# Dealing the context's attention units among the latent ones, and taking two norms as columns

## The chip, the cores and the metric

One core of one Trainium2 chip runs the whole kernel. The metric is device time in microseconds (us) from the start to the end of one execution; lower is better. A profiled execution also gives a span, from the core's first instruction to its last, and a trace of every instruction on TensorE (PE, with its weight loads as PEld), VectorE (DVE), ScalarE (ACT), GpSimd (POOL) and the DMA queues, of which SP's is one.

## The reference

The network has two layers, over a prefix of 256 context tokens and 1024 latent tokens, 1024 features wide. Layer 0 is windowed attention, layer 1 a Mamba-2 mixer. The part that matters here is layer 0 and the norm in front of layer 1:

```python
u = rms_normalize(h) * (1.0 + scale[:, None]) + shift[:, None]      # before each layer, h latent or context
# layer 0, a block of 128 latent queries: keys of up to 3 neighbouring blocks and all 256 context keys
s = jnp.einsum('bqkgd,bskd->bkgqs', qb, kb).astype(jnp.float32) * scale
p = sink_softmax(s, sink_kg, mask).astype(vb.dtype)
o = jnp.einsum('bkgqs,bskd->bqkgd', p, vb)
# the context's queries: the 256 context keys alone
s = jnp.einsum('bqkgd,bskd->bkgqs', q_c, k_c).astype(jnp.float32) * scale
p = sink_softmax(s, sink_kg, None).astype(v_c.dtype)
# both: gate, output projection, gated residual
y = (o * jax.nn.silu(g)) @ w_out
h = h + gate[:, None] * y
```

`rms_normalize` multiplies each token by one over the square root of the mean of its squares plus 1e-6. There are 16 query heads in 4 groups; each group shares one key/value head.

## The kernel before

Features lie on the partitions, tokens on the free axis. The tokens are three tiles: tile 0 and tile 1 are latent tokens 0 to 511 and 512 to 1023, tile 2 is the context (256). Every fp32 product is made of three fp32r matmuls, from a high part and a low part of each operand (`mm3`, lines 220 to 226: a high weight by high data, a low weight by high data and a high weight by low data). The low parts are made by subtraction: for weights on GpSimd (`split_w`, line 212), after a cast on ScalarE (line 210).

**Units.** Attention runs over 40 units, one for each of 10 blocks of 128 queries (blocks 0 to 3 are tile 0, 4 to 7 tile 1, 8 and 9 the context) and each of 4 key/value heads `j`. A unit has a front (`att_front`): the scores `S` of 4 query heads on TensorE (lines 670 for latent keys, 671 for context keys), mask and row minimum on VectorE (674), the exponential on ScalarE (676). It has a back (`att_back`): for each block of keys, 4 transposes into `pt` (695), a copy to `ph` on ScalarE (699), the low part `pl` on VectorE (700), and two matmuls into `pv` (701, 702). Then come two transposes of the reciprocal sums (708), the gate (709), the copy `co` (711), the sum `ot` (714), the product with the gate on GpSimd (715), and high and low part of the result (717, 718). A latent unit has 4 or 5 blocks of keys, a context unit has 2. The front of the next unit is traced ahead of the back of this one (`AHEAD = 1`).

**Fillers.** Between the key blocks of the units stand parts of projections that don't depend on them. `tick`, called once per key block, hands out `total * seen / count` parts. Each part is 3 matmuls with a moving operand of 512 columns (256 for tile 2's output), 8 parts (24 matmuls) make one projection into the single PSUM bank `pj`. Each projection loads two half weights on SP's queue and splits them. The list is in three stages: beside the 8 context units 5 projections (`QC`) of tile 1's queries; beside the 16 units of tile 0 the other 3 queries and 8 gates of tile 1; beside the 16 units of tile 1 the output projections of tile 2 and then of tile 0 (`out_steps`). Query projections end in the rotary rotation (lines 532 to 553), gate projections in a tanh and one VectorE instruction (571, 572).

**Norms.** After its 8 output projections a tile has the residual stream in DRAM (`h_d`) and the sum of squares in `acc`. `fin` makes the norm: `rstd` multiplies `acc` by a matrix of ones on TensorE (256), so that all 128 partitions hold the sum, then takes a square root on ScalarE (258) and a reciprocal on VectorE (259) of the whole tile. `modulate` then reads `h_d` back in 8 pieces, through two buffers `h1`, and makes high and low part of the normed input of layer 1 (291 to 293). Both are done for tile 2 and for tile 0 during or at the end of the units of tile 1.

**After the units** come the output projections of tile 1 (8, on alternating banks), a small projection for the time steps of the context (`dt_context`), the norm of tile 1 (`rstd_last`, which takes sums of squares as columns, line 796, and the power -1/2 on GpSimd, line 800) and layer 1.

**What sets the order.** The code is traced once; a scheduler then orders each engine's instructions by its own estimate of their times, by priority (fillers have a lower one) and by a few forced orders (`issue_after`). The result is a fixed sequence per engine; each engine takes its instructions in that order and waits at one whose inputs are not there.

## Time and profile before

| | us |
|---|---|
| runs of the kernel before: median (lowest to highest, 3 runs) | 1783.06 (1781.8 to 1784.47) |
| the profiled execution's own time | 1781.34 |
| its span | 1779.6 |
| TensorE busy in the span | 1727.1 (97%) |
| VectorE, ScalarE, GpSimd busy | 1172.5, 840.8, 808.4 |
| units of the context, from the first score matmul to the last units' end | about 260 to 336 |
| units of tile 0 | to about 508 |
| units of tile 1 | to about 701 |

The stage times are read off the trace where the gate's product (line 709) of the last unit of each stage runs. Busy TensorE is not TensorE at its peak: a matmul's record includes the time it takes to pass through the array, so one that stands alone shows 0.39 us where a stream of the same ones takes one every 0.23 us. The busy time of the weight loads (PEld), one for each matmul and of 0.19 us for most, tells more about how dense the stream is.

### The profile page before, as it was taken

The numbers are of one execution on the slowest core, as the hardware profiler recorded it, in microseconds if no ns is written. First come the engines' busy times: TensorE is split into PE (matmuls) and PEld (weight loads), VectorE is DVE, ScalarE is ACT, GpSimd is POOL, SyncE is SP. The second block draws the span as 40 slices with busy tenths as digits, with TensorE's granted clock in tenths as the row PEclk, the third lists the DMA queues.
The fourth block names the chain that finished last, engine by engine and source line by source line (L and its number), as shares of the span: only waits on it lengthen the run. The fifth ranks groups of instructions, "written<-read, shape, count | busy, mean of one in ns | idle before, by whom it ended". The sixth has DMA issues, their size and how long they took to land.

```text
span 1779.6 us, 28767 instructions
## 1 busy us (share of the span) xinstructions
PE 1727.1 (97%) x10115; PEld 1479.3 (83%) x10115; DVE 1172.5 (66%) x2174; ACT 840.8 (47%) x1769; POOL 808.4 (45%) x1070
## 2 busy tenths in 40 slices
PE   6999998999999899999999999999999999999997
PEld 3797767788889787789898898989889898987886
DVE  3563436787777766585776758677675866876643
ACT  3532226677778766453443434344343443443533
POOL 2441117654456465403455463635545464554222
PEclk9999999999999999999999999999999999999999
DMA  8758866553445444412333333233333333565533
GB/s 302 284 148 258 265 190 148 124 130 85 101 119 130 119 143 151 164 47 64 86 78 90 80 79 83 78 92 72 95 81 80 83 77 88 167 174 161 179 106 119
DMA packets 261617, 227.89 MB, mean 128 GB/s; under 512 B 84704, under 2 KB 201312, under 8 KB 260448
## 3 DMA queue, kind: packets, MB, share of 16 engines
q1 hardware_dynamic: 227408, 207.40, 39.8%
q0 software_dynamic: 34064, 18.65, 5.8%
q8 instruction: 80, 1.31, 0.3%
q14 instruction: 65, 0.53, 0.1%
HBM read 191.14 MB, written 35.13 MB: 127 GB/s over the span
## 4 chain that ended last, share of the span: by engine, by line
PE 85%; DVE 5%; issue 3%; DMA 3%; ACT 2%; POOL 1%; SPq 0%; DVEq 0%; POOLq 0%; ACTq 0%
PE pj L1182 19%; PE pj L1218 10%; PE pj L224 6%; PE pj L226 6%; PE pj L225 6%; PE pj L1664 4%; PE psD L1199 4%; PE pt L695 3%; PE psX L1365 3%; PE psD L1278 2%; PE pv L702 2%; PE pv L701 2%; PE S L670 2%; PE psX L1338 1%; PE psX L1337 1%
## 5 line engine op out<-in xcount | busy, mean ns | idle before, releaser
L224 PE MATMUL pj<-uH,wh 128*128 128x512 f32 (+1 forms) x572 | 212.6, 372 | 5.5 <-DVE rope_b L533 2.3
L226 PE MATMUL pj<-uH,wl 128*128 128x512 f32 (+1 forms) x572 | 200.2, 350 | 0.1
L225 PE MATMUL pj<-uL,wh 128*128 128x512 f32 (+1 forms) x572 | 199.7, 349 | 0.0
L212 POOL TENSOR_TENSOR wl<-wr,wh 128x512 fp32r<-128x512 f32 x92 | 121.3, 1321 | 98.5 <-ACT wh L210 97.0
L1182 PE MATMUL pj<-uH,wl 128*128 128x512 f32 x480 | 163.3, 407 | 0.0
L1182 PE MATMUL pj<-uH,wh 128*128 128x512 f32 x480 | 163.1, 411 | 0.0
L1182 PE MATMUL pj<-uL,wh 128*128 128x512 f32 x480 | 162.3, 408 | 0.0
L700 DVE TENSOR_TENSOR pl<-pt,ph 128x512 fp32r<-128x512 f32 x168 | 114.2, 687 | 60.6 <-ACT ph L699 59.8
L1218 PE MATMUL pj<-wh,uL 128*128 128x256 f32 x512 | 152.3, 297 | 0.0
L1218 PE MATMUL pj<-wh,uH 128*128 128x256 f32 x512 | 152.0, 297 | 0.0
L1218 PE MATMUL pj<-wl,uH 128*128 128x256 f32 x512 | 151.8, 296 | 0.0
L224 PEld LDWEIGHTS pj<-uH,wh 128*128 128x128 f32 x572 | 108.2, 189 | 32.9 <-issue 8.4
L674 DVE CUSTOM_DVE_ANT_0 sm<-S,mask,nsink 128x640 f32<-128x640 f32 (+2 forms) x160 | 118.8, 772 | 25.4 <-PE S L671 13.6
L210 ACT CAST wh<-wr 128x512 fp32r<-128x512 f32 (+1 forms) x132 | 84.8, 645 | 94.9 <-PE pj L225 68.0
L699 ACT CAST ph<-pt 128x512 fp32r<-128x512 f32 x168 | 97.4, 585 | 63.7 <-PE pt L695 58.1
L676 ACT ACTIVATE sm<-sm,nm 128x640 f32<-128x640 f32 (+2 forms) x160 | 118.6, 742 | 11.7 <-DVE nm L674 11.4
L226 PEld LDWEIGHTS pj<-uH,wl 128*128 128x128 f32 x572 | 108.0, 189 | 16.5 <-issue 1.7
L225 PEld LDWEIGHTS pj<-uL,wh 128*128 128x128 f32 x572 | 108.5, 190 | 12.4 <-issue 2.5
L1255 POOL TENSOR_TENSOR xw<-xn,dtdec 128x256 f32<-128x256 f32 x144 | 91.7, 641 | 55.3 <-PE psD L1278 31.4
L1373 POOL TENSOR_TENSOR ss<-ss,half 128x1 f32<-128x1 f32 x64 | 43.0, 672 | 160.3 <-ACT y L1372 160.2
L1331 POOL TENSOR_TENSOR xs<-xn,sk 128x256 f32<-128x256 f32 x64 | 46.2, 722 | 134.7 <-DVE sk L1329 134.6
L1182 PEld LDWEIGHTS pj<-uL,wh 128*128 128x128 f32 x480 | 90.4, 188 | 18.3
(415 smaller groups left out, 4994.0 us busy)
## 6 DMA issues: line engine op xcount, KB each, us to landing
fd<-acs SPq DMA_DIRECT2D x64, 256.0 KB, 4.9
bd<-acs SPq DMA_DIRECT2D x64, 256.0 KB, 4.9
wr<-w_x SPq DMA_DIRECT2D x31, 512.0 KB, 3.7
wr<-w_sk SPq DMA_DIRECT2D x24, 512.0 KB, 4.1
wr<-wg SPq DMA_DIRECT2D x44, 256.0 KB, 4.4
qs<-q POOLq DMA_DIRECT2D x40, 256.0 KB, 3.9
wr<-wo SPq DMA_DIRECT2D x40, 256.0 KB, 2.7
wada<-w_ad SPq DMA_DIRECT2D x8, 1024.0 KB, 6.4
```

Of the source, the lines that this page charges most:

```text
L210: nc.scalar.copy(h, raw)
L212: (eng or nc.vector).tensor_tensor(l, raw, h, op=ALU.subtract)
L224: self.nc.tensor.matmul(ps, lh, rh, start=first and i == 0, stop=False)
L225: self.nc.tensor.matmul(ps, lh, rl, start=False, stop=False)
L226: self.nc.tensor.matmul(ps, ll, rh, start=False, stop=last and i == n - 1)
L674: nc.vector.tensor_tensor_reduce(out=sm[:, :W], in0=Sv, in1=self.mask[:, m0 : m0 + W], scale=-SCALE, scalar=self.nsink[:, 4 * j + r : 4 * ...
L676: nc.scalar.activation(sm[:, :W], sm[:, :W], AF.Exp, bias=nm[:, r : r + 1], scale=-1.0, accum_out=sums[:, r : r + 1])
L699: nc.scalar.copy(ph, ptf)
L700: nc.vector.tensor_sub(pl, ptf, ph)
L1182: nc.tensor.matmul(raw[:, 512 * i : 512 * i + 512], l[:, k, :], r[i][:, k, :], start=k + y == 0, stop=k == KT - 1 and y == 2)
L1218: nc.tensor.matmul(pj[:, c], l, r[:, k, :], start=c % 2 + q + k + y == 0, stop=c % 2 == 1 and q == 1 and k == 3 and y == 2)
L1255: nc.gpsimd.tensor_tensor(xw, X(st, c).rearrange("p (r h) -> p r h", r=R), self.dtdec[:, c, hd(d, g)].unsqueeze(2).broadcast_to([P, R, HP] ...
```

## The change

Three things are changed, and two constants with them.

1. The list of units. The 8 context units no longer come first: each is followed by two units of tile 0. The fillers beside these 24 units are one list (8 queries, then 8 gates), handed out by weight: a key block of a context unit counts twice (`load`). `QC` is no longer used, and the second list's `count` is 2 larger, so that a few of its steps are left for the flush after the last unit.
2. The norms of tiles 2 and 0. The sums of squares are taken as columns (one matmul with one column per 128 tokens), scaled on VectorE, raised to -1/2 by GpSimd; in a second step, matmuls with the columns broadcast as weights and the identity as moving operand spread them over the partitions, and ScalarE copies the result. The square root, the reciprocal and the matmul by ones are gone there. The modulation (`rescale`) becomes a generator of 8 steps, and `aside` takes one of them after each filler part; what is left after the last unit is done at once.
3. `dt_context` is put behind the matmuls of the fourth output projection of tile 1, as these were traced last.

```diff
-SLACK = (0, 0, 0)
+SLACK = (0, 2)
...
+            def rescale(r):
+                for k in range(KT):
+                    h = t(self.po, [P, n], F32, "h1")
+                    nc.sync.dma_start(h, self.h_d[k][i])
+                    self.modulate(1, h, r, i, k)
+                    yield
+
             def fin():
                 yield
                 p = self.po
-                r = rstd_last(p) if i == 1 else self.rstd(p, ps, st["acc"], n, D)
+                if i == 1:
+                    r = rstd_last(p)
...
+                    return
+                nb = n // P
+                pn = t(ps, [P, 512], F32, "pj")
+                for b in range(nb):
+                    nc.tensor.matmul(pn[:, b : b + 1], st["acc"][:, b * P : (b + 1) * P], self.ones[:, 0:1], start=True, stop=True)
+                rc = t(p, [P, 4], F32, "rc")
+                nc.vector.tensor_scalar(out=rc[:, :nb], in0=pn[:, :nb], scalar1=1.0 / D, scalar2=EPS, op0=ALU.mult, op1=ALU.add)
+                nc.gpsimd.tensor_tensor(rc[:, :nb], rc[:, :nb], self.mhalf[:, :nb], op=ALU.pow)
+                yield
+                pr = t(ps, [P, 512], F32, "pj")
+                for b in range(nb):
+                    nc.tensor.matmul(pr[:, b * P : (b + 1) * P], rc[:, b : b + 1].broadcast_to([P, P]), self.ident, start=True, stop=True)
+                r = t(p, [P, n], F32, "sqa")
+                nc.scalar.copy(r, pr[:, :n])
                 self.alloc_u(i)
-                for k in range(KT):
-                    if i == 1:
-                        h = st[k]
-                    else:
-                        h = t(p, [P, n], F32, "h1")
-                        nc.sync.dma_start(h, self.h_d[k][i])
-                    self.modulate(1, h, r, i, k)
+                side.append(rescale(r))
...
-        fill = {2: pr[:QC], 0: pr[QC:], 1: out_steps(2) + out_steps(0)}
-        total = {2: QC * PARTS, 0: (16 - QC) * PARTS, 1: 16 * PARTS + 2}
-        units = [(i, j, b) for i, blocks in ((2, range(8, 10)), (0, range(0, 4)), (1, range(4, 8))) for b in blocks for j in range(KV)]
+        fill = [pr, out_steps(2) + out_steps(0)]
+        total = [16 * PARTS, 16 * PARTS + 4]
+        one = [(0, j, b) for b in range(0, 4) for j in range(KV)]
+        units = []
+        for x in range(8):
+            units += [(2, x % KV, 8 + x // KV)] + one[2 * x : 2 * x + 2]
+        units += [(1, j, b) for b in range(4, 8) for j in range(KV)]
         nkb = lambda b: 2 if b >= 8 else 2 + min(b + 2, 8) - max(b - 1, 0)
+        load = lambda b: 2 if b >= 8 else 1
...
             nonlocal cur, nxt
-            seen[i] += 1
...
+            q = int(i == 1)
+            seen[q] += load(b)
...
+                    aside()
...
         tick(True)
+        while side:
+            aside()
...
-            self.dt_context()
+                if n == 3:
+                    late = next(x for x in reversed(nc.cur_bb.bb.instructions) if x.engine == mybir.EngineType.PE)
+            with self.tc.issue_after(late):
+                self.dt_context()
```

What the scheduler makes of it is seen best at three places. The first is TensorE in the stretch of the first units. `S` are scores, `pt` transposes, `pv` the products with the values, and `pj<-uH,wh` and its like are fillers. Before, in the middle of the context's units:

```order
L708 MATMUL pt_2919<-ident_63,rs_2763 128x128 x2
L671 MATMUL S_2944<-kHH_185_729,qs_2931 128x256
L671 MATMUL S_2944<-kL_189_733,qz_500_2571 128x256
L701 MATMUL pv_2881<-ph_2907,v_728 128x512
L671 MATMUL S_2950<-kHH_185_729,qs_2931 128x256
L671 MATMUL S_2950<-kL_189_733,qz_500_2571 128x256
L224 MATMUL pj_3010<-uH_168_632,wh_2814 128x512
L225 MATMUL pj_3010<-uL_169_633,wh_2814 128x512
L226 MATMUL pj_3010<-uH_168_632,wl_2816 128x512
```

In the change, a few units after the start:

```order
L695 MATMUL pt_2950<-ident_63,sm_2774 128x128
L224 MATMUL pj_2853<-uH_168_632,wh_2693 128x512
L225 MATMUL pj_2853<-uL_169_633,wh_2693 128x512
L226 MATMUL pj_2853<-uH_168_632,wl_2695 128x512
L670 MATMUL S_3000<-kHH_187_731,qs_2993 128x256
L671 MATMUL S_3000<-kHH_187_731,qs_2993 128x256
L670 MATMUL S_3000<-kL_190_734,qz_500_2571 128x256
L671 MATMUL S_3000<-kL_190_734,qz_500_2571 128x256
L702 MATMUL pv_2921<-pl_2942,v_728 128x512
L695 MATMUL pt_2967<-ident_63,sm_2750 128x128
```

Before, the fillers stand in runs of 9 to 24 between the short context units (the run whose first three rows are shown has 12); in the change most runs are of 3, one part per key block, with latent scores (line 670) between them.

The second place is TensorE at the end of the last unit, where tile 0's norm stands (`pj<-sqa,ones` before, lines 831 and 838 of the changed kernel now). Before:

```order
L256 MATMUL pj_8202<-sqa_7174,ones_68 128x512
L701 MATMUL pv_8137<-ph_8174,v_728 128x512
L702 MATMUL pv_8137<-pl_8175,v_728 128x512
L708 MATMUL pt_8249<-ident_63,rs_8048 128x128 x2
L701 MATMUL pv_8137<-ph_8196,v_728 128x512
L702 MATMUL pv_8137<-pl_8197,v_728 128x512
L224 MATMUL pj_8330<-uH_1386_5741,wh_8294 128x512
```

In the change:

```order
L708 MATMUL pt_8200<-ident_63,rs_8048 128x128 x2
L226 MATMUL S_8433<-uH_1386_5741,wl_8336 128x512
L701 MATMUL pv_8131<-ph_8188,v_728 128x512
L702 MATMUL pv_8131<-pl_8189,v_728 128x512
L831 MATMUL pj_8220<-ones_68,sqa_7191 128x1 x4
L838 MATMUL pj_8228<-ident_63,rc_8225 128x128 x4
L224 MATMUL S_8389<-uH_1386_5741,sm_8328 128x512
```

The norm's first matmul has moved from before the last products to behind them, and its second one, which needs the power, stands right behind the first with nothing between. The third place is GpSimd's queue at the same moment, in the change (`ot` is the last unit's result, `rc` the power):

```order
L780 TENSOR_TENSOR sqa_7191<-sqa_7191,ut_8217 128x512
L752 TENSOR_TENSOR sm_8317<-ph_8314,sm_8316 128x512
L212 TENSOR_TENSOR wl_8423<-wr_8419,wh_8421 128x512
L715 TENSOR_TENSOR ot_8206<-ot_8206,sgt_8007 128x256
L834 TENSOR_TENSOR rc_8225<-rc_8225,mhalf_72 128x4
L718 TENSOR_TENSOR uL_1387_5742<-ot_8206,uH_1386_5741 128x2x128
```

The power stands behind the last sum of squares, two weight splits and the last unit's gate product; before, GpSimd had no part in this norm.

More of the change, by code (lines that the diff above doesn't have):

```diff
@@ L814, in fin @@
                 p = self.po
[L815 to L823 removed]
+                if i == 1:
+                    r = rstd_last(p)
+                    self.alloc_u(i)
+                    for k in range(KT):
+                        self.modulate(1, st[k], r, i, k)
+                    return
@@ L831, in attention, with aside @@
         nkb = lambda b: 2 if b >= 8 else 2 + min(b + 2, 8) - max(b - 1, 0)
-        count = {i: sum(nkb(u[2]) for u in units if u[0] == i) - SLACK[i] for i in range(3)}
-        seen, done = [0, 0, 0], [0, 0, 0]
-        self.last = []
+        load = lambda b: 2 if b >= 8 else 1
+        count = [sum(nkb(u[2]) * load(u[2]) for u in units if (u[0] == 1) == q) + SLACK[q] for q in range(2)]
+        seen, done = [0, 0], [0, 0]
+        self.last, side = [], []
         cur = nxt = None
+        def aside():
+            if side and next(side[0], "end") == "end":
+                side.pop(0)
@@ L847, in tick @@
                         nxt = None
-                        src = next((fill[y] for y in (2, 0, 1)[(2, 0, 1).index(i) :] if fill[y]), None)
+                        src = next((fill[y] for y in range(q, 2) if fill[y]), None)
                         if src:
```

6 lines of the change are left out of this document (3 added, 3 removed).

## The prediction

> **What bounds the kernel now.** I read first the page's busy times, then busy time by stretches of the attention stage, then TensorE's waits.
>
> ```profile
> PE 1727.1 (97%) x10115; PEld 1479.3 (83%) x10115; DVE 1172.5 (66%) x2174; ACT 840.8 (47%) x1769; POOL 808.4 (45%) x1070
> ```
>
> TensorE is the bound as a whole, and the change takes no work worth naming from it. So what can be gained is TensorE's own slack, in the stretches that the change touches. The view of stretches has, after the length, each engine's busy time with its number of instructions (PE, weight loads, VectorE, ScalarE, GpSimd), then the granted clock:
>
> ```profile
> 255.00:275.00 20.00, 17.16 (x79) 13.83 (x78) 10.50 (x39) 10.03 (x30) 7.78 (x13) 0.83 0.65 152
> 275.00:348.00 73.00, 65.50 (x353) 52.95 (x352) 54.00 (x141) 45.74 (x124) 51.66 (x74) 1.00 0.58 137
> 340.00:380.00 40.00, 39.80 (x240) 34.10 (x239) 34.17 (x80) 29.58 (x68) 23.89 (x37) 1.00 0.51 123
> 348.00:560.00 212.00, 209.96 (x1286) 181.92 (x1285) 162.50 (x351) 159.58 (x354) 118.03 (x175) 1.00 0.45 112
> 586.00:620.00 34.00, 29.09 (x148) 22.77 (x148) 28.04 (x58) 25.64 (x55) 13.75 (x22) 0.95 0.46 120
> 698.00:712.00 14.00, 11.50 (x61) 8.89 (x60) 11.83 (x12) 10.62 (x17) 8.26 (x7) 1.00 0.76 244
> ```
>
> The second column shows the density best. In the units of tile 0 (348 to 560) weight loads fill 181.92/212 = 85.8% of the time and TensorE is 99% busy: that is what a full stream looks like here. Three stretches fall short. Around the context's units (275 to 348) the loads fill 72.5%; at a density of 85.5% (between the rows of 340 to 380 and 348 to 560) the same work would take 52.95/0.855 = 61.9 us, so 11.1 us are lost. The start (255 to 275) loses 20 - 13.83/0.855 = 3.8, tile 2's norm (586 to 620) 34 - 26.6 = 7.4, and the end of the units with tile 0's norm (698 to 712) 14 - 10.4 = 3.6. Together 26 us, or 1.5% of the span. TensorE's waits name who is late:
>
> ```profile
> PE pv L702 <- DVE pl L700: 4.8, 12, 1.8
> PE pv L701 <- ACT ph L699: 3.1, 5, 1.6
> PE pj L224 <- DVE rope_b L533: 2.3, 3, 1.7
> PE pt L957 <- DVE al L945: 1.8, 1, 1.8
> PE pj L224 <- ACT sqa L258: 1.6, 2, 0.8
> PE pj L224 <- DVE h L769: 1.1, 1, 1.1
> ```
>
> The first two are the chain of a unit's key block, the third the one bank `pj` that waits for the rotation, the others the norms and the time-step projection.
>
> Part of the loss is the clock. Three windows of 3.41 us (clock 0.50) ran at half of it, which costs about 1.7 us each where TensorE had work:
>
> ```profile
> 259.88:263.29 3.41, 2.01 (x14) 1.47 (x13) 2.39 (x9) 2.12 (x7) 0.46 (x1) 1.00 0.27 101
> 263.29:266.70 3.41, 3.41 (x15) 2.81 (x13) 2.16 (x9) 1.41 (x6) 2.11 (x6) 0.50 1.05 281
> 270.11:273.52 3.41, 3.41 (x17) 3.13 (x16) 1.47 (x7) 1.93 (x7) 0.83 (x2) 0.50 0.68 184
> 604.62:608.03 3.41, 1.72 (x10) 1.30 (x10) 2.86 (x6) 1.72 (x4) 0.18 (x1) 1.00 0.43 150
> 608.03:611.44 3.41, 3.41 (x13) 2.73 (x12) 3.41 (x9) 2.13 (x6) 0.40 (x2) 0.50 0.06 19
> 707.02:710.43 3.41, 1.64 (x14) 1.35 (x13) 3.41 (x5) 2.62 (x5) 1.46 (x2) 1.00 1.01 339
> ```
>
> The first and the fourth row are windows just ahead of a fall (busy 2.01 and 1.72 us). The last row had only 1.64 us, and no half clock followed; so an idle stretch of this size sometimes costs the window and sometimes not.
>
> **The change part by part. A, the dealt units.** Nothing is added or removed; 24 units and 16 projections are the same work. Before, a context unit with two key blocks had 5 filler parts, in long runs, and its short chain (scores, row minimum, exponential, transposes, `ph`, `pl`, products) had too little other attention work beside it. In the change a unit of 4 or 5 key blocks stands on both sides, and one part of 3 fillers stands behind nearly each key block. What speaks for the dense rate in that mix is the row of 340 to 380: units of tile 0 with query projections beside them, at 85.3% loads and TensorE 99.5% busy. What speaks against it is VectorE, since all 8 query projections now fall beside the first 12 units instead of the first 13:
>
> ```profile
> L532 DVE TENSOR_TENSOR qf<-pj,cos 128x512 f32<-128x512 f32 x8 | 5.5, 690 | 6.5 <-PE pj L226 6.4
> L533 DVE STREAM_SHUFFLE rope_b<-pj 128x512 f32<-128x512 f32 x8 | 5.9, 736 | 0.0
> L535 DVE TENSOR_TENSOR qf<-qf,rope_b 128x512 f32<-128x512 f32 x8 | 5.9, 737 | 0.0
> L553 DVE TENSOR_TENSOR ql<-qf,qh 128x512 fp32r<-128x512 f32 x8 | 8.9, 1118 | 4.5 <-ACT qh L552 4.4
> ```
>
> That is 3.3 us for one projection and 26 us for all. VectorE's whole load from 275 to 560 is 54.0 + 162.5 = 216.5 us; in 274 us (285 less 11) it would be 79% busy, more in the first half, and 85% (34.17 of 40) was still dense in the row above. The start should stay: the first unit has nothing before it in both orders, and its weights arrive as late as before. So A gains between 0 (the chain of the context units stays as it is) and 11.1 + 3.8 = 14.9; I take 9, four fifths of the 11.1, nearer to the dense rows because most of the stretch will look like them.
>
> **B, tile 2's norm.** Removed: one matmul by ones, a square root with its two table loads, one reciprocal; added: columns, a power, a spread.
>
> ```profile
> L258 ACT ACT_TABLE_LOAD x2 | 2.6, 1283 | 0.0
> L259 DVE RECIPROCAL sqa<-sqa 128x256 f32<-128x256 f32 x1 | 1.8, 1752 | 1.9 <-ACT sqa L258 1.9
> L259 DVE RECIPROCAL sqa<-sqa 128x512 f32<-128x512 f32 x1 | 3.4, 3352 | 0.7 <-ACT sqa L258 0.7
> 748.47 0.16 DVE L799 TENSOR_SCALAR rc<-pt 128x4 f32<-128x4 f32 x1 [2.21 <-PE pt L796]
> 748.72 1.04 POOL L800 TENSOR_TENSOR rc<-rc,mhalf 128x4 f32<-128x4 f32 x1 [2.27 <-DVE rc L799]
> 749.79 0.69 DVE L802 TENSOR_TENSOR ut<-ident,rc 128x512 f32<-128x512 f32 x1 [1.16 <-POOL rc L800]
> 598.85 0.39 PE L225 MATMUL pj<-uL,wh 128*128 128x512 f32 x1
> 599.07 0.39 PE L226 MATMUL pj<-uH,wl 128*128 128x512 f32 x1
> 618.29 0.50 PE L224 MATMUL pj<-uH,wh 128*128 128x512 f32 x1 [1.07 <-DVE h L769]
> ```
>
> The large loss here is in the last rows (fillers, 0.22 us apart, then none): from 599 to 618 TensorE had no filler at all, because the next residual tile `h1` waited for the 8 pieces of the modulation to pass through the same two buffers, with VectorE busy 28.04 of 34 us. Spreading the pieces over filler parts does not lift this. The next projection but one still asks for its `h1` after all 8, and the changed order shows about two units of attention without fillers there, as against some one and a half before. What is better: two projections instead of one can run before that point (24 more matmuls, 5 us of work), VectorE loses 1.75 us of reciprocal and ScalarE two table loads (1.28 each), and the pieces are further apart. What is worse: the spread waits for the power on GpSimd (0.16 + 1.04 and the hops, 1.3 us on free engines by the three rows of tile 1's norm), with 16 instructions of attention between. B gains between 7.4 (all of the loss) and -2 (a longer stretch without fillers, another half clock); I take 2, nearer to no gain since the cause stays.
>
> **C, tile 0's norm and the end of the units.** Before, its matmul stood before the last products and 168 fillers behind could run after a wait of 0.8 us. Now TensorE's order has the column sums behind the last product and the spread right behind these, so all of tile 1's output projection waits behind line 838 for GpSimd. The chain from the last product on is `co`, two `ot`, the gate product, the power:
>
> ```profile
> L711 ACT COPY co<-pv 64x512 f32<-64x512 f32 x40 | 23.3, 583 | 26.2 <-PE pv L702 25.9
> L714 DVE TENSOR_TENSOR ot<-pv,co 64x256 f32<-64x256 f32 x80 | 33.0, 412 | 6.8 <-ACT co L711 6.2
> L715 POOL TENSOR_TENSOR ot<-ot,sgt 128x256 f32<-128x256 f32 x40 | 30.7, 767 | 27.2 <-DVE ot L714 25.2 <-DVE sgt L709 1.7
> L780 POOL TENSOR_TENSOR sqa<-sqa,ut 128x512 f32<-128x512 f32 x13 | 17.2, 1320 | 4.5 <-ACT sqa L773 3.1 <-ACT ut L776 1.1
> L752 POOL TENSOR_TENSOR sm<-ph,sm 128x512 fp32r<-128x512 f32 x8 | 11.8, 1472 | 7.4 <-ACT sm L751 6.7 <-PE pj L225 0.7
> L212 POOL TENSOR_TENSOR wl<-wr,wh 128x512 fp32r<-128x512 f32 x72 | 93.4, 1299 | 48.4 <-ACT wh L210 47.7 <-DVE sums L683 0.3
> ```
>
> On free engines 0.58 + 2 x 0.41 + 0.77 + 1.04, with some 0.5 of hops, is 3.7 us. If GpSimd still has the last sum of squares and both splits before it, 1.32 + 1.47 + 1.30 + 0.77 + 1.04 and hops are 6.4. Then come the spread, its copy on ScalarE and two casts of weights there before fillers flow: 1 to 2 us more, less about 1 of useful matmuls in between. The new loss is 3.7 to 7.4, and 1.7 more if the gap brings a half clock; I take 6, because a gap of 4 us is longer than each one that brought a half clock above. Of before's 3.6 us, 1.8 were `dt_context`'s wait for `al`, which goes away since it now runs behind all 168 fillers (38 us). C costs 6 - 3.6 = 2.4, with bounds of 0.1 and 5.5. Tile 0's modulation, 8 pieces, then runs under those 38 us, as it ran under them before; without that cover it would cost what the stretch of tile 2 shows.
>
> The Trainium skill ("TensorE: Matmul & The Clock Gate", part 1 on the HAM clock gate) says that the clock falls to half after one idle window of about 3.4 us. The rows above show a fall after windows in which TensorE was busy for 1.72 to 2.01 us and none after 1.64; so the measurement is stricter at times. By the page alone C would pay the 1.7 only if the gap covers a whole window, and the sum would be 1.7 lower. The skill ("SBUF — State Buffer", the section on its two separate sides) also says that a GpSimd instruction and a VectorE instruction with two SBUF inputs shut each other out for a whole instruction. In the changed order VectorE has two such subtractions behind the column's scaling, about when the gate product and the power run; by that rule C's chain would be longer by up to one of them, still inside C's bounds.
>
> **The sum.** -9 - 2 + 2.4 = -8.6 against the profiled execution's 1781.34 gives 1772.7. That execution lies 1.7 below the median of the runs shown, so for the median 1774. A measurement of this kernel can tell about 0.2%, 3.6 us, from no change.
>
> **The rivals.** *The gain of A is smaller than the cost of C.* If the context units keep their own chain wherever they stand, A gives 2 and C 5.5: 1783 - 2 - 2 + 5.5 = 1784.5, no change. For it: the chain AHEAD by one unit is the same. Against it: the row of 340 to 380. *VectorE becomes the bound of the first half (slower).* All rotations beside 12 units. The dealt work is 52.95 + 181.92 = 234.9 us of loads; if its first half ran at 76% instead of 85.5%, which is near what 275 to 348 had, it would take 117.4/0.76 - 117.4/0.855 = 17 us more than dense; less the 11.1 lost before that is +6, with B and C 6.4, so 1789. It decides once VectorE is over about 95% busy in the first 12 units; the 85% of 340 to 380 speaks against it, the 74% (54.0 of 73) in the context's stretch says that VectorE was not the bound there either. *All three gaps close.* A 14.9, B 7.4, C 0: 1761. For it: the order has fillers almost everywhere in A; against it, the stretch without fillers in B and the wait in C. That the change does not do what it says is out: the order shows the dealt units and the columns.
>
> **How the numbers follow.** The forecast has 0.69 (1766 to 1779.4), the first rival 0.13 (around 1780 to 1786), VectorE's bound 0.07 (1787 and above), the full gain 0.11 (below 1766). Range 1763 to 1783. Faster by over 0.2% is the forecast and the full gain, 0.80; within 0.2% most of the first rival, 0.12; slower the rest of it and VectorE's bound, 0.08.
>
> **What would show it.** In the changed profile: loads at 82 to 86% from the second unit to the end of tile 0's units, which should come some 9 us earlier; no table load between the exponentials; still a stretch of 15 us or more without fillers behind tile 2's norm; TensorE idle for 4 us or more before line 838 at the end of the units, with GpSimd's power as the releaser. The prediction is wrong if TensorE waits for `pl` and `ph` as often among the dealt units as before, if the gap at line 838 is over 8 us, or if it is under 2.

## The result: slower, where faster was predicted

The changed kernel takes 1794.24 us (median of 4 runs, 1793.03 to 1796.72), the kernel before beside it 1783.76 (1781.80 to 1785.00). The ratio is 1.0066, with a 95% interval of 1.0053 to 1.0078: 11.8 us slower by the ratio, 10.5 between the two medians. 1774 was predicted, with a range of 1763 to 1783 and a chance of 0.80 for faster. The prediction is wrong in sign, by 20 us.

The profiled execution of the changed kernel took 1794.95 us, with a span of 1793.3 against 1779.6. Four points that both traces have cut the span into stretches. The end of tile 0's units is where the product of line 709 of the last of them begins (510.1 us before, not the 508 of the table further up):

| stretch (us) | before | after | difference |
|---|---|---|---|
| start to first score | 259.7 | 258.8 | -0.9 |
| first score to the end of tile 0's units | 250.4 | 249.6 | -0.8 |
| to the last value product (tile 1's units) | 190.4 | 191.1 | +0.7 |
| to layer 1's first product | 52.9 | 64.4 | +11.6 |
| to the end | 1026.2 | 1029.3 | +3.1 |

The page's busy times show that TensorE got 9 us busier with almost the same work, as it would at a lower clock (its mean is 0.988 against 0.993):

```profile
PE 1736.1 (97%) x10135; PEld 1485.2 (83%) x10135; DVE 1169.1 (65%) x2174; ACT 839.5 (47%) x1765; POOL 810.2 (45%) x1072
```

The view of stretches (length; busy time and instructions of TensorE, weight loads, VectorE, ScalarE, GpSimd; clock; DMA), at the places shown of before:

```profile
255.00:275.00 20.00, 15.90 (x69) 12.07 (x68) 7.90 (x25) 8.57 (x22) 7.52 (x10) 0.91 0.52 144
275.00:348.00 73.00, 68.14 (x387) 56.56 (x386) 58.69 (x140) 49.69 (x122) 45.77 (x67) 0.98 0.51 122
348.00:508.00 160.00, 157.71 (x896) 132.47 (x895) 120.86 (x278) 117.89 (x273) 90.64 (x137) 1.00 0.46 113
586.00:625.00 39.00, 36.11 (x197) 30.22 (x198) 30.28 (x63) 26.13 (x59) 19.11 (x29) 0.96 0.42 110
699.00:713.00 14.00, 8.21 (x32) 6.75 (x31) 6.92 (x10) 6.92 (x12) 8.41 (x7) 0.63 0.90 302
```

The first 73 us are denser (loads 56.56/73 = 77.5%, 72.5% before), the rest of tile 0's units is thinner (82.8%, 84.3% before in the same 160 us). The slack was spread, and little of it removed. The last row is the worst: after the last value product TensorE is busy 8.21 of 14 us, at a mean clock of 0.63. Of TensorE's waits, grouped (us in total, times, the longest), these are the ones that matter here; others that both kernels have are left out:

```profile
PE pv L702 <- DVE pl L700: 7.0, 21, 2.4
PE pj L838 <- POOL rc L834: 4.0, 1, 4.0
PE pv L701 <- ACT ph L699: 3.1, 2, 2.3
PE pt L805 <- DVE ut L802: 2.3, 1, 2.3
PE S L224 <- ACT sm L751: 1.7, 1, 1.7
PE psD L1699 <- ACT fd L1349: 1.7, 1, 1.7
PE psX L1390 <- DVE y L1404: 1.6, 1, 1.6
```

The wait for `pl` has grown from 4.8 us in 12 waits to 7.0 in 21, and the second, fourth and fifth rows, 8 us, are new. Behind the long waits of these rows stand stretches at half clock. Pairs of windows, the one with the wait and the one behind it:

```profile
319.37:322.79 3.42, 1.22 (x7) 1.07 (x8) 3.08 (x4) 0.02 (x1) 2.12 (x2) 1.00 0.62 145
322.79:326.20 3.41, 3.41 (x9) 2.64 (x8) 0.84 (x3) 1.06 (x3) 0.20 (x1) 0.50 0.48 152
...
698.25:701.67 3.42, 2.07 (x15) 1.76 (x13) 0.85 (x3) 1.72 (x3) 2.20 (x3) 1.00 0.71 217
701.67:711.91 10.24, 5.80 (x17) 4.73 (x18) 5.17 (x7) 4.51 (x8) 6.88 (x6) 0.50 0.95 322
756.29:759.70 3.41, 1.11 (x6) 0.47 (x5) 2.12 (x3) 2.09 (x2) 0.00 (x0) 1.00 0.04 17
759.70:763.11 3.41, 3.41 (x7) 1.46 (x8) 1.77 (x3) 0.72 (x2) 0.00 (x0) 0.50 0.83 231
1626.69:1630.10 3.41, 0.97 (x4) 0.30 (x2) 2.65 (x6) 1.84 (x4) 0.00 (x0) 1.00 0.91 300
1630.10:1636.92 6.82, 5.97 (x14) 4.75 (x15) 6.22 (x13) 2.76 (x7) 4.09 (x6) 0.50 0.60 174
```

With two more at 268 and 620, half clock between the first score and the last 20 us lasts 30.7 us in this execution and 10.2 us in the one of before. Half of the difference, 10 us, is what this can have cost at most, out of the 13.7 by which the spans differ; for part of it TensorE stood still anyway (it is busy 5.80 of the 10.24 us behind 701.67).

Two of these places in detail. GpSimd's queue at the end of the units:

```profile
700.15 1.27 POOL L752 TENSOR_TENSOR sm<-ph,sm 128x512 fp32r<-128x512 f32 x1 [1.22 <-ACT sm L751]
701.37 1.26 POOL L212 TENSOR_TENSOR wl<-wr,wh 128x512 fp32r<-128x512 f32 x1
702.59 0.72 POOL L715 TENSOR_TENSOR ot<-ot,sgt 128x256 f32<-128x256 f32 x1
703.27 1.04 POOL L834 TENSOR_TENSOR rc<-rc,mhalf 128x4 f32<-128x4 f32 x1
```

The power stands behind two weight splits and the last unit's gate product, as its order says. TensorE's rows there:

```profile
699.14 0.40 PE L702 MATMUL pv<-pl,v 128*128 128x512 f32 x1
699.37 0.95 PE L831 MATMUL pj<-ones,sqa 128*128 128x1 f32 x8
704.37 2.08 PE L838 MATMUL pj<-ident,rc 128*128 128x128 f32 x8 [4.05 <-POOL rc L834]
708.18 0.79 PE L224 MATMUL S<-uH,sm 128*128 128x512 f32 x1 [1.74 <-ACT sm L751]
```

The spread (L838) waits 4.05 us, then runs 2.08 us at half clock, and the first output projections wait for their weights' late halves. At tile 1's norm, VectorE:

```profile
757.58 1.23 DVE L1135 TENSOR_TENSOR wl<-wr,wh 128x1024 fp32r<-128x1024 f32 x1 [2.47 <-ACT wh L1131]
758.73 0.69 DVE L802 TENSOR_TENSOR ut<-ident,rc 128x512 f32<-128x512 f32 x1
```

L802, which TensorE waits for, now stands behind layer 1's weight split (L1135), which waits for a cast (L1131) and that for a transfer. Before, it ran at 749.79, right behind the power, and the split came 3.3 us later (L1100 at 753.10).

### The profile page after: what moved, and what is told of

It is laid out like the page before. It is cut to its first block, busy times and chain, and to the rows that moved or that the text cites. A ratio compares the mean times of both kernels' runs of the same rounds, so it can differ in the third digit from the quotient of the medians.

```text
span 1793.3 us, 28795 instructions
## 1 busy us (share of the span) xinstructions
PE 1736.1 (97%) x10135; PEld 1485.2 (83%) x10135; DVE 1169.1 (65%) x2174; ACT 839.5 (47%) x1765; POOL 810.2 (45%) x1072
## 4 chain that ended last, share of the span: by engine, by line
PE 85%; DVE 6%; issue 3%; DMA 3%; ACT 2%; POOL 1%; SPq 0%; DVEq 0%; POOLq 0%; ACTq 0%
PE pj L1217 19%; PE pj L1253 10%; PE pj L224 6%; PE pj L226 5%; PE pj L225 5%; PE pj L1699 5%; PE psD L1234 4%; PE psX L1400 3%; PE pt L695 3%; PE psD L1313 2%; PE pv L702 2%; PE psD L1699 2%; PE psX L1373 1%; PE psX L1372 1%; PE pv L701 1%
## 5 line engine op out<-in xcount | busy, mean ns | idle before, releaser
L212 POOL TENSOR_TENSOR wl<-wr,wh 128x512 fp32r<-128x512 f32 x92 | 121.7, 1325 | 116.9 <-ACT wh L210 111.7
```

Of the source, the lines that this page charges most:

```text
L212: (eng or nc.vector).tensor_tensor(l, raw, h, op=ALU.subtract)
```

## The experiments

Theory one: the end of the units costs the time, by waits and the half clock behind them; the dealing gains almost nothing. Its rivals: the dealing itself costs (theory two), or the moved time steps are free. All kernels compute the same outputs. Ratios are to the kernel before on the same chip, whose median lay between 1783.5 and 1783.9 in each set. The last two columns are means over a kernel's runs: the granted clock, and span times clock, an estimate of the span that the kernel would have without half clock (too low where TensorE stood still at half clock).

| kernel | us | ratio (95% interval) | clock | span x clock |
|---|---|---|---|---|
| before (102 runs) | 1783.6 | 1 | 0.9927 | 1769 |
| changed kernel | 1794.2 | 1.0066 (1.0053 to 1.0078) | 0.9883 | 1772 |
| units_only | 1781.9 | 0.9991 (0.9983 to 1.0000) | 0.9926 | 1767 |
| norms_only | 1790.4 | 1.0041 (1.0026 to 1.0057) | 0.9898 | 1771 |
| dt_only | 1789.7 | 1.0036 (1.0022 to 1.0051) | 0.9912 | 1772 |
| no_dt | 1788.4 | 1.0019 (1.0009 to 1.0030) | 0.9904 | 1769 |
| dt_order | 1787.6 | 1.0023 (1.0009 to 1.0036) | 0.9914 | 1770 |
| dt_both | 1786.7 | 1.0019 (1.0006 to 1.0032) | 0.9914 | 1770 |
| spread_late | 1787.6 | 1.0029 (1.0015 to 1.0042) | 0.9919 | 1772 |
| warm | 1789.7 | 1.0041 (1.0029 to 1.0053) | 0.9920 | 1774 |
| units_alt | 1777.4 | 0.9959 (0.9945 to 0.9973) | 0.9930 | 1763 |
| norm2 | 1785.3 | 1.0009 (0.9999 to 1.0019) | 0.9918 | 1769 |
| norm2_ut | 1777.7 | 0.9963 (0.9950 to 0.9975) | 0.9932 | 1764 |
| late_nodt | 1787.4 | 1.0014 (1.0005 to 1.0022) | 0.9916 | 1770 |
| best | 1774.4 | 0.9950 (0.9934 to 0.9966) | 0.9930 | 1760 |
| before_alt | 1780.8 | 0.9986 (0.9974 to 0.9999) | 0.9933 | 1768 |

### The change taken apart

**units_only**: the dealing alone.

```diff
-SLACK = (0, 0, 0)
+SLACK = (0, 0)
...
-        fill = {2: pr[:QC], 0: pr[QC:], 1: out_steps(2) + out_steps(0)}
+        fill = [pr, out_steps(2) + out_steps(0)]
...
+        for x in range(8):
+            units += [(2, x % KV, 8 + x // KV)] + one[2 * x : 2 * x + 2]
+        units += [(1, j, b) for b in range(4, 8) for j in range(KV)]
```

The diff is against the kernel before; the norms and the time steps stay as they were there.

> Only the dealt units: the norms of tiles 2 and 0 and the context's time steps are as in the kernel before. Theory one (the end of the units is what costs, the dealing itself gains almost nothing): the first score to tile 0's last unit takes about 249.6 us instead of 250.4, the last value product to layer 1's first product stays at 53 us, and the time is 0 to 2 us under the kernel before, 1782 to 1784. Theory two (the dealing costs, because the query projections' rotations stand on VectorE beside the units): 3 us or more above the kernel before.

Measured 0.9991: 1.6 us faster, at the edge of what can be told from none. Theory two falls; the dealing does no harm, and little good.

**norms_only**: the kernel before with the new norms of tiles 2 and 0.

```diff
-SLACK = (0, 0, 0)
+SLACK = (0, -2, 0)
...
-                r = rstd_last(p) if i == 1 else self.rstd(p, ps, st["acc"], n, D)
...
+                nc.gpsimd.tensor_tensor(rc[:, :nb], rc[:, :nb], self.mhalf[:, :nb], op=ALU.pow)
+                yield
...
+                side.append(rescale(r))
```

> Only the norms of tiles 2 and 0 as columns with their modulation spread, in the old order of the units, and the context's time steps at their old place. Theory one: the stretch from the last value product to layer 1's first product grows from 53 to about 60 us (the wait for GpSimd's power of about 4, the half clock behind it of 3 to 5, the weights' copy of 1.7, less nothing since the context's wait for al stays), the time is 1789 to 1792. Theory two (the dealing costs): under 1786.

1790.4, as theory one had it, and the last stretch took 58.4 us. But TensorE did not wait for the power: the context's products stood ahead of the spread, and it waited for their weights (L983, the products at their old place):

```profile
PE pt L983 <- ACT wdth L963: 3.9, 1, 3.9
```

The reason, as I read the code, is the one bank `pj`: the column sums and the spread both use it, so the projections that need it too cannot come between. No run changed the bank alone.

**dt_only**: the kernel before with the time steps moved.

```diff
+                if n == 3:
+                    late = next(x for x in reversed(nc.cur_bb.bb.instructions) if x.engine == mybir.EngineType.PE)
-            self.dt_context()
+            with self.tc.issue_after(late):
+                self.dt_context()
```

> Only the context's time steps moved from ahead of tile 1's norm to behind the fifth output projection's start. Theory one says that the move brings back the 1.8 us wait for al and costs at tile 1's norm, where VectorE's layer 1 weight split comes ahead of the spread of the power (2.3 us and a half clock of 1.7): the time is 0 to 3 us above the kernel before, 1783 to 1787. Theory three (the move only gains, its 1.8 us): 1782.

6.4 us slower, more than theory one had and far from the gain that I had booked. Two waits take the place of the 1.8 us for `al`:

```profile
707.82 0.80 PE L224 MATMUL pj<-uH,sm 128*128 128x512 f32 x1 [2.62 <-ACT uH L717]
...
753.67 1.10 PE L805 MATMUL pt<-ut,ones 128*128 128x512 f32 x2 [2.52 <-DVE ut L802]
```

The first is for the last unit's result (`uH`, L717). In the kernel before it comes no earlier:

```profile
710.00 0.39 ACT L717 CAST uH<-ot 128x256 fp32r<-128x256 f32 x1
```

There the context's products were what TensorE did meanwhile, after the wait for `al`. By these rows the wait for `al` hid a later one.

**no_dt**: the changed kernel without the move.

```diff
-            with self.tc.issue_after(late):
-                self.dt_context()
+            self.dt_context()
```

> The changed kernel with the context's time steps back at their old place. Theory one: it gets back the 2.3 us and the half clock of 1.7 at tile 1's norm and pays again the 1.8 for al, unless al is there earlier: 1790 to 1793 against 1794 of the changed kernel. Theory three (the move only gains): 1795 to 1797.

1788.4, lower than both expected: by the ratios the move costs 1.0066 - 1.0019, or 8.4 us, of the changed kernel's 11.8, by the medians 6.0 of 10.5. Its waits at the norm of tile 1 are gone; a wait of 4.1 for the context's weights remains.

### The moved time steps mended

**dt_order**: dt_only, with VectorE's order at tile 1's norm mended.

```diff
-                nc.vector.tensor_tensor(dg, self.ident.unsqueeze(1).broadcast_to([P, 4, P]), rc.unsqueeze(2).broadcast_to([P, 4, P]), op=ALU.mult)
+                self.dg = nc.vector.tensor_tensor(dg, self.ident.unsqueeze(1).broadcast_to([P, 4, P]), rc.unsqueeze(2).broadcast_to([P, 4, P]), op=ALU.mult)
...
-                nc.vector.tensor_sub(w["l"], raw, w["h"])
+                with self.tc.issue_after(self.dg.ins) if g == 0 else ExitStack():
+                    nc.vector.tensor_sub(w["l"], raw, w["h"])
```

> The kernel before with the context's time steps moved, and with layer 1's two low weight parts queued on VectorE behind the spread of tile 1's power (the instruction that was late by 2.5 us in the run with the move alone). Theory one (the move costs through VectorE's order at tile 1's norm and through the half clock that its gap brings): the gap of 2.5 us ahead of the power's spread product is gone and the time is 2.5 to 4 us under the run with the move alone, so 1785.5 to 1787.5. Theory two (that run was slow by chance windows of half clock alone, not by the order): 1788.5 to 1791.

1787.6, just above theory one's range. The gap ahead of L805 is gone (L802 runs at 751.74, the weight splits behind it); the gain is 1.0036 to 1.0023, with intervals that overlap, so its size is not settled.

**dt_both**: and layer 1's first weights later.

```diff
                 if n == 3:
...
+                    cast = next(x for x in reversed(nc.cur_bb.bb.instructions) if x.engine == mybir.EngineType.Activation)
+                    with self.tc.issue_after(cast):
+                        self.first_w()
...
         self.dts = t(q, [P, 5 * P], F32, "dt")
+
+    def first_w(self):
+        nc, t, a, q = self.nc, self.t, self.a, self.pdt
         raw = t(q, [P, KT, P], F32, "wf")
```

> As the last, and layer 1's first weights are loaded and split only behind the fourth output projection, so that their cast no longer stands on ScalarE ahead of the cast of the output weights. Theory one: the second gap of the move (2.6 us ahead of the first output projection's second half) goes as well, another 2.6 and some half clock: 1781 to 1784, at or under the kernel before. If the gap is only handed on to the next late weight, 1785 to 1787.

1786.7, a miss for theory one. The wait was handed on, to the next late weight:

```profile
PE S L224 <- ACT sm L751: 3.0, 1, 3.0
```

So neither mend makes the move pay, and the two ratios, 1.0023 and 1.0019, can't be told apart. The rows of the waits say that TensorE needs other work there; the context's 24 products, about 2.8 us at the 0.117 us that one takes in the kernel before, are such work. That this is all that the move costs is not shown: late_nodt, below, speaks against it.

### The spread, and the clock by itself

**spread_late**: the changed kernel with tile 0's spread behind two output projections.

```diff
-                r = t(p, [P, n], F32, "sqa")
+                r = t(p, [P, n], F32, "sqa") if i == 2 else t(self.pa, [P, n], F32, "qs")
...
-        total = [16 * PARTS, 16 * PARTS + 4]
+        total = [16 * PARTS, 16 * PARTS + 3]
...
-        while side:
-            aside()
...
+                if n == 1:
+                    mm = next(x for x in reversed(nc.cur_bb.bb.instructions) if x.engine == mybir.EngineType.PE)
+                    with self.tc.issue_after(mm):
+                        next(cur, "end")
+                    while side:
+                        aside()
```

> The changed kernel with tile 0's norm spread behind two output projections of tile 1 instead of ahead of them, and its modulation behind that. Theory one (the wait for GpSimd's power on TensorE's path and the half clock behind it are the largest part of the loss): the 4.05 us gap is gone, no window of half clock of 10 us stands behind the last value product, the last value product to layer 1's first product takes 56 to 58 us instead of 64, and the time is 1785 to 1788 against 1794. A rival (the wait only moves, to the output weights or the first banks): 1790 or more.

1787.6, and 57.0 us for the stretch: as expected. The wait for the power was on the path, and the spread need not be.

**warm**: the wait stays, TensorE is kept busy in it.

```diff
                 pr = t(ps, [P, 512], F32, "pj")
+                for _ in range(14 if i == 0 else 0):
+                    nc.tensor.matmul(pr, oH[0][:, 0, :P], oH[0][:, 1, :], start=True, stop=True)
                 for b in range(nb):
```

> The changed kernel with 14 products of 128x512 that nobody reads between the column sums and the spread of tile 0's norm: 3.2 us of work in the same 4 us gap, so the wait stays and only the idleness goes. Theory one (half clock is most of the loss at that place): no window of half clock there, the spread's 8 passes take about 1 us instead of 2.1, and the time is 4 to 5 us under the changed kernel, 1789 to 1790.5. A rival (the wait itself is the loss and the clock follows something else): 1793 to 1796.

```profile
699.08 3.47 PE L838 MATMUL pj<-uH 128*128 128x512 f32 x14 [1.92 <-DVE rc L833]
702.38 1.05 PE L840 MATMUL pj<-ident,rc 128*128 128x128 f32 x8
```

The 14 products that nobody reads ended later than the power would have been there: the spread begins 5.2 us behind the column sums' end (702.38 - 697.16), 4.05 in the changed kernel. Still the kernel is 4.6 us faster (1.0066 to 1.0041), its spread takes 1.05 us instead of 2.08, and no half clock stands at this place. Span times clock rose by 2 us while the mean clock went from 0.9883 to 0.9920. So the idleness, not the wait, was the larger cost, if the ratios are taken as they stand: their intervals just touch, and the profile of warm lacks half clock at other places too (at 268 and 323 us, which the edit does not touch).

**late_nodt**: spread_late, with the time steps at their old place.

```diff
-            with self.tc.issue_after(late):
-                self.dt_context()
+            self.dt_context()
```

> The changed kernel with tile 0's spread behind two output projections of tile 1, as in the run before, and the context's time steps at their old place. Theory one (the context's products were what TensorE had to do while the last unit's output and the late halves of the weights were on their way, so moving them away opened those waits): against the run with the spread late alone the waits of 1.5 us for the late weights and of 1.9 us at tile 1's norm go, and the time is 3 to 6 us lower, 1781.5 to 1784.5. Rival (the place of the context's products does not matter): 1786.5 to 1788.5.

1787.4: a miss. The wait at tile 1's norm shrank (0.7 us after 1.9), the one for the late weights stayed (1.3 after 1.5), and the stretch took 56.9 us again, with two windows of half clock at 702.5 and 750.3. The ratios, 1.0014 and 1.0029, can't be told apart. So where the spread is late, the place of the context's products makes no difference that can be seen: what the move costs depends on what else stands there. Both windows of half clock stand behind column sums (the last section comes back to that).

### The dealt units and tile 2's norm

**units_alt**: units_only with query and gate projections in turn.

```diff
+        pr = [pr[x // 2 + 8 * (x % 2)] for x in range(16)]
         fill = [pr, out_steps(2) + out_steps(0)]
```

> The dealt units alone, with query and gate projections in turn as fillers, so that the rotations of the 8 query projections (3.3 us each on VectorE) spread over all 24 units instead of the first 12. Theory one (the dealing gained only 0.8 to 1.6 because pl now waits behind the rotations on VectorE): TensorE's waits for pl between 258 and 510 us fall from 5.1 us to 2 or less, the stretch from the first score to tile 0's last unit gets 2 to 4 us shorter, and the time is 1778 to 1780. Theory two (there was little idle time to win: 9.1 us of the 235, most of it at other places): no change against the dealt units alone, 1781 to 1783.

1777.4, below theory one's range. The waits for `pl` from 258 to 510 us, in the kernel before, in the changed kernel (the row of units_only is the same) and here:

```profile
PE pv L702 <- DVE pl L700: 1.4, 4, 0.8
PE pv L702 <- DVE pl L700: 5.1, 12, 2.4
PE pv L702 <- DVE pl L700: 2.4, 11, 0.4
```

The longest had stood behind one of the rotation's subtractions. VectorE in the changed kernel:

```profile
317.99 2.92 DVE L553 TENSOR_TENSOR ql<-qf,qh 128x512 fp32r<-128x512 f32 x1 [0.78 <-ACT qh L552]
320.83 1.27 DVE L700 TENSOR_TENSOR pl<-pt,ph 128x512 fp32r<-128x512 f32 x2
```

It took 2.92 us, where the median of the 8 is 0.71, while GpSimd worked without a pause (L715, L684, L212 from 318.04 to 320.35). In units_alt the slowest of the 8 took 0.87. The Trainium skill ("SBUF — State Buffer", its section on two separate sides) says that a VectorE instruction with two SBUF inputs and a GpSimd instruction that reads SBUF shut each other out for a whole instruction. These rows fit that in kind, with three GpSimd instructions for one; but no run took GpSimd's work away alone, so this cause is argued, not shown. That the bunched order costs is shown, 4.5 us between the medians and 5.7 by the ratios. The waits for `pl` are 2.7 of it; where the rest comes from, and whether the gates' ends have a part in it, which the turn spreads as well, was not taken apart.

**norm2**: units_only with the column norm for tile 2 alone. The diff is against the changed kernel and shows what keeps the old norm for tile 0; the time steps are at their old place as well.

```diff
+                if i == 0:
+                    r = self.rstd(p, ps, st["acc"], n, D)
+                    self.alloc_u(i)
+                    for _ in rescale(r):
+                        pass
+                    return
                 nb = n // P
```

> The dealt units, and the column norm with its spread pieces for tile 2 alone; tile 0's norm and the context's time steps as in the kernel before. If this part gains the 2 us that I gave it: 1779 to 1781. If the stretch without fillers stays as long as the order has it (99 rows of attention without a filler against 72 with the old norm): 1782 to 1785.

1785.3 against 1781.9: this part costs 3.2 us by the ratios. TensorE stood without a filler for 24.7 us (609.81 to 634.47), 20.0 in units_only and 19.2 before.

**norm2_ut**: the pieces in other buffers.

```diff
-                    h = t(self.po, [P, n], F32, "h1")
+                    h = t(self.po, [P, n], F32, "ut" if i == 2 else "h1")
```

> As the last, but tile 2's pieces of the modulation are loaded into the buffers of the squares (three of them) instead of the two of the residual tiles, so that the output projections' own residual tiles no longer wait for the eight pieces. Theory one (the two shared buffers are what leaves TensorE without fillers behind tile 2's norm): the stretch without fillers goes (the order has none of over 24 rows), no half clock falls between 600 and 625 us, and the time is 5 to 8 us under the last run, 1776 to 1779. Rival (VectorE, busy 28 of 34 us there, is the bound): within 2 us of the last run.

1777.7, 7.6 us below norm2. There is no half clock from 586 to 625 us, and TensorE is busy 36.88 us of 39. The stretch in norm2, whose mean clock was 0.91:

```profile
586.00:625.00 39.00, 35.51 (x186) 28.91 (x184) 28.08 (x61) 24.95 (x56) 17.16 (x26) 0.91 0.44 108
```

and in norm2_ut:

```profile
586.00:625.00 39.00, 36.88 (x206) 31.02 (x205) 31.72 (x69) 28.31 (x63) 20.43 (x31) 1.00 0.55 142
```

VectorE was busier (31.72 of 39) and did not bound it. The longest time without a filler behind the norm is 3.7 us. The two buffers of `h1`, which the pieces share with the output projections' residual tiles, were the cause. The tag used in their place, that of the projections' squares, has three buffers; whether one more for `h1` would have done was not tried.

**best**: norm2_ut with the projections in turn, and **before_alt**: the kernel before with nothing but the turn.

```diff
+        pr = [pr[x // 2 + 8 * (x % 2)] for x in range(16)]
```

> The dealt units with query and gate projections in turn, tile 2's column norm with its pieces in the squares' buffers, everything from tile 0's norm on as in the kernel before. If the two gains are independent (6.2 us of the turn and dealing, 4.2 of the norm over the dealt units alone): 1772 to 1775. If they are the same idle time won twice: 1776 to 1778.

> The kernel before with nothing but the query and gate projections in turn; the units stay in their old order. If the turn alone is what gains (the rotations leave VectorE free in the first units, whatever these are): 1777 to 1780, like the dealt units with the turn (1777.4). If the dealing is needed as well (the context units' short chain stays uncovered in their run): 1781 to 1784.

best takes 1774.4 us, 0.9950 (0.9934 to 0.9966) of the kernel before: the two gains add, and it beats both kernels. before_alt lies between its two expectations at 0.9986. The turn alone gains 2.5 us, the dealing alone 1.6, both (units_alt) 7.3: the dealing pays once the rotations are spread. With these intervals it is not settled that both give more than the sum of the two.

## Why the prediction was wrong

Four kernels that each add one part to the last give the price of every term (differences of the ratios, times 1783.6):

| step | predicted | measured |
|---|---|---|
| A, dealt units (units_only) | -9 | -1.6 |
| B, tile 2's norm (norm2) | -2 | +3.2 |
| C, tile 0's norm and its pacing (no_dt) | +4.2 | +1.8 |
| C, time steps moved (changed kernel) | -1.8 | +8.4 |
| sum | -8.6 | +11.8 |

Each price is good to 1.5 to 3 us, if the intervals are added as independent: A is at the edge of nothing, the +1.8 can't be told from nothing, B and the last step can. Between the medians the last step is 6.0 and the sum 10.5. And the prices of C hold in this order only: with the spread late (spread_late) the changed kernel is 6.6 us faster too, and there moving the time steps back made no difference that can be seen (late_nodt).

**A.** The failed step is "most of the stretch will look like" the dense rows. The density of weight loads put the loss at 11.1 us and took no account of the mix of the work: TensorE's idle time from 275 to 510 us was only 235 - 225.86 = 9.1 us in the view of stretches. The dealing alone left 7.3 of it (units_only) and moved the waits from `ph` and the rotation (2.8 and 2.3 us before, 0.8 and 0.3 then) to `pl` (1.4 before, 5.1 then). I saw VectorE's 26 us of rotations, priced them as a mean share of 79%, and dismissed it. A mean says nothing of the single key block whose `pl` stands behind a run of rotations. The slower rival named the right engine with the wrong size. That dealing could pay is shown by units_alt: with the rotations spread, 4.8 us are idle and the gain is 7.3 us, near the 9. The sign: loads were 77.5% and then 82.8%, where 82 to 86% was the mark, and TensorE waited for `pl` more often, not less (12 times, 4 before).

**B.** The cause was read rightly (the two buffers of `h1`, a stretch of 15 us or more without fillers: 24.9 us came; the table loads are gone, as said), and the conclusion not drawn: if the cause stays and the pieces are spread out, the buffers are held longer. I took a gain of 2, with the cheaper norm and the two projections ahead of that point on its side; the other bound, a loss of 2 for a longer stretch and another half clock, was nearer to the loss of 3.2 that was measured.

**C.** The gap ahead of the spread was 4.05 us with the power as the releaser, as said, and its half clock came too, three windows of it (10.24 us) where one was priced. The failed step is "`dt_context`'s wait for `al`, which goes away since it now runs behind all 168 fillers". I asked what the moved products wait for and not what they cover: the wait for the last unit's result or the weights' late halves (2.62, 1.74 us) took its place in the rows. That this is the whole price of the move is argued from the rows and not shown; what else is in the 8.4 us stays open. And the reordering of VectorE at tile 1's norm (2.3 us and a half clock), 50 us behind the edit, was in the order that I had and was not looked at.

**The clock.** The sum priced one half clock of 1.7 us. Over all runs the mean clock fell from 0.9927 to 0.9883; times a span of 1790 that is 7.9 us, at most two thirds of the loss by the ratio. The step that failed is costing a gap by its length, with one window of half clock for the whole kernel.

**Layer 1's +3.1** is probably not the change's. The profiles of all fourteen experiments, like that of the changed kernel, show half clock of 3.4 or 6.8 us between 1610 and 1637 us, before_alt among them, which leaves layer 1 as it was; the one profile of before does not, though the same two waits are there. So that execution was probably a lucky one at this place; there is no second profile of it to show that.

## What to carry to other kernels

Before work is moved away from a wait, look at what TensorE would do in its place until the next late input: a wait that ends last may only be standing in front of another. Price a gap of 2 to 4 us on TensorE at its length plus the half clock that may stand behind it; in the one gap of this kernel where it was tried, products that nobody reads were worth 4.6 us. And where pieces are spread out to be gentle, count how long they hold the buffers that the next work needs: here one other tag for `h1` and one line that alternates the fillers turned the dealt units and the column norm from 1.6 us of loss into 8.9 of gain.

## What the runs showed of the hardware

*The same gap costs or does not, by its phase against the clock's windows.* The two waits at layer 1's end, in the profile of before, without a fall:

```profile
1614.95:1618.36 3.41, 2.00 (x9) 1.24 (x7) 1.62 (x3) 1.43 (x2) 0.00 (x0) 1.00 0.93 294
1618.36:1621.77 3.41, 1.75 (x8) 1.31 (x8) 3.41 (x7) 2.19 (x7) 0.55 (x1) 1.00 0.74 267
```

and in units_only, where the windows cut them elsewhere:

```profile
1614.67:1618.09 3.42, 2.23 (x11) 1.55 (x10) 0.55 (x1) 1.14 (x2) 0.00 (x0) 1.00 0.77 250
1618.09:1621.50 3.41, 1.16 (x4) 0.75 (x5) 3.41 (x8) 2.02 (x8) 0.55 (x1) 1.00 0.83 279
1621.50:1624.92 3.42, 3.42 (x10) 2.66 (x9) 3.24 (x10) 0.97 (x3) 1.54 (x3) 0.50 0.71 238
```

The Trainium skill ("TensorE: Matmul & The Clock Gate", part 1) says that the window runs freely and a kernel's cold stretches vary with its phase. No run here sets the phase; what the runs show is that the kernel before alone has spans from 1776.5 us at a mean clock of 0.996 to 1789.3 at 0.989. Where the page asks for an idle window, the windows ahead of a fall shown in this document were busy for 0.97 us or more of 3.41.

*A fall can come behind a window that looks busy.* In late_nodt the clock fell after a window that the profile shows 2.68 us busy:

```profile
746.88:750.29 3.41, 2.68 (x21) 2.28 (x20) 0.16 (x1) 0.87 (x2) 0.46 (x1) 1.00 0.56 114
750.29:753.71 3.42, 3.42 (x9) 1.77 (x7) 0.93 (x2) 1.08 (x2) 0.57 (x1) 0.50 0.69 277
```

Sixteen of its passes are tile 1's column sums, products over one column (128x1). Without them it would be busy for 0.98 us. The same count over the windows of all sixteen profiles, from 252 us to 15 us before the end, with the 3.41 us grid on which the half clocks begin: if the one-column products are left out, each of the 35 windows at full clock that were busy for less than 1.5 us brought a fall, of those between 1.5 and 2.1 us 21 did and 57 did not, and above that none did. If they are counted in, falls stand behind windows of 2.17 and 2.68 us too. So the column form of a norm seems to be dear in clock. The bounds were read off the same windows, and no run changed the column sums alone.
